# Conditioning matmuls in batches of two k-tiles, and a last output projection that closes one row tile after the other

## The chip, the cores and the metric

The kernel runs on one core of one Trainium2 chip. The time is device microseconds of one execution, the median of several runs. The engines named here are PE (TensorE: matmuls, with PEld for its weight loads), DVE (VectorE), ACT (ScalarE), POOL (GpSimd) and SP (SyncE, which issues the DMAs). Weights come from HBM into SBUF; matmuls write to PSUM, which has eight banks of 128x512 f32.

## The reference

Two layers work on 256 latent and 256 context tokens of width 2048. Cut to what matters here:

```
mod = silu(c) @ ada_w + ada_b              # 2048 -> 6144: shift, scale, gate; also for c_ctx
h   = rms_norm(x, pre_norm) * (1 + scale) + shift
p   = split_columns(h @ w_in)              # one input projection for all branches
att = gqa_attention(q, k, v) * silu(g)     # 8 heads of 128: rows 0 to 7 of the mix (128 columns each)
rw  = rwkv_output(scan fwd + scan bwd) * silu(g)   # 8 heads of 64: rows 8 to 11
pool= pool_mixer(...) * silu(g)            # rows 12 to 15
y   = concat(att, rw, pool) @ w_out        # 2048 -> 2048
x   = x + gate * rms_norm(y, post_norm)
```

The recurrent branch runs four head pairs, the context before the latent tokens; a pair's latent scan starts from the state in which its context scan ends. In the second layer only the latent tokens' output is needed. All is float32.

## The kernel before

The program is written by a list scheduler in Python. Workers (generators: `ada_work`, `main_work`, `front_work`, `back_work`, `scan_work`, `post_work` and others) yield operations; the planner estimates when each could start and takes the earliest, by a priority in steps of 40 ns. What comes out is one fixed order for each engine, and at run time every engine goes through its own order. Buffers are tiles of pools, by class: `wf` (weights as loaded), `sp` (weights split in two), `wa` (conditioning weights), `acc`, `pr`, `scan`, `att`, `ada` (the eight PSUM banks), `y` and so on. PHASES says how many of each class are kept free for it, and the most that it may hold.

The big projections multiply in float32r. A weight tile lands in `wf`, ACT makes a rounded copy (CAST `sp<-wf`), DVE the remainder (TENSOR_TENSOR `sp<-wf,sp`), and three matmuls for each output tile add up the products (high x high, high x low, low x high). This stream, `acc<-h,sp` for the input projections and `acc<-sp,h` for the output projections, is the worker `main`.

The conditioning vectors come from `ada_work`. After the first tiles of layer 0 it walks through 8 parts of 4 x 256 columns, with 16 k-tiles each. A k-tile has two weight tiles `wa` of 128x512, and each makes two matmuls `ada<-wa` with a stationary operand of two columns, into the four strips of 32 rows of one PSUM bank. Before, one k-tile was multiplied as soon as its two tiles were there, in the order in which they were loaded. The array has another form there than in the 128x128 matmuls; the planner holds `ada` matmuls back by 3000 ns of its own time when that form would have to change:

```
HOLD = {None: 1000.0, "ada": 3000.0}
```

The last output projection is two steps, `("out", 1, 1, 0)` and `("out", 1, 1, 1)`: columns 0 to 1023 over all 16 k-tiles, then columns 1024 to 2047. Each holds four PSUM banks (two column tiles `n` by two row tiles `t`). The k-tiles go in the order KMIX, in which the recurrent branch's rows come last: `MIX_ORDER = [0, 1, 2, 3, 6, 7, 4, 5]`. A k-tile's matmuls can't be placed until its row of the mix is there (`self.until("m", l, s, k // 2)`), so in the first step the last two k-tiles (row pair 5, with the last head pair's scan) come after the end of the last scan, and the whole second step after these.

The scan of a head pair (`scan`) has four steps. In each, PE makes `scan<-rf`, ACT copies the result to `sm`, PE makes `scan<-sm,rb`, ACT copies to `rf`, PE makes `scan<-rf,rb`, and DVE updates state and output (`ts`). After the fourth a group norm follows (a reduction, a square on ACT, a `rsqrt` of small DVE steps) and the matmuls `scan<-c,ts`, from which the last rows of the mix are made. `pr<-tp,rb` and `pr<-tp` (32x32) belong to `fin`, which prepares a unit for its scan.

`post_work` closes a projection. For each PSUM bank DVE multiplies by the gate (`y<-acc,y`) and ACT sums the squares (`y,q<-acc`). When all eight are there it takes one `rsqrt` for both row tiles, and for each of eight tiles DVE makes the output (SCALAR_TENSOR_TENSOR `y<-y,q`) and SP writes it.

## Time and profile before

| | us |
|---|---|
| median of 3 runs | 1771.61 (1769.43 to 1776.53) |
| the profiled execution | 1770.03 |
| its span, first to last instruction | 1768.1 |
| PE busy in the span | 1675.5 (95%) |
| DVE busy | 1350.8 (76%) |
| ACT busy | 926.8 (52%) |

The profiled execution's own time is 1.9 us above its span. Busy shares are means over stages with different limits, so a stage is read from a table of its stretch. The ends of matmuls are modelled: their starts are the firm numbers, and the time from one start to the next is what a matmul costs in a stream. A trace shows a program's float32 matmul of this kind as two records (the float32r ones as one): 4 `ada<-wa` of the program are 8 in the trace.

### The profile page before, as it was taken

What the parts mean: (1) busy time and instruction counts of PE and PEld (TensorE: products, weight loads), DVE (VectorE), ACT (ScalarE), POOL (GpSimd) and SP (SyncE); (2) the same over time, 40 slices, a digit from 0 to 9 for tenths busy, and PEclk for the clock granted to TensorE, in tenths of its full rate; (3) what the DMA queues carried; (4) which work ended last, traced back from release to release, by engine and by line L of the source; (5) the groups of instructions that cost most, each with busy time, mean ns of one, the idle gap of its engine ahead of it and who ended that gap; (6) DMA issues with size and microseconds to landing.
All of it is one profiled execution on the core that took longest, in us unless ns stands there. A gap on an engine that the chain in (4) does not pass through costs nothing.

```text
span 1768.1 us, 38232 instructions
## 1 busy us (share of the span) xinstructions
PE 1675.5 (95%) x13658; PEld 1330.3 (75%) x13658; DVE 1350.8 (76%) x4249; ACT 926.8 (52%) x2278; POOL 16.0 (1%) x93
## 2 busy tenths in 40 slices
PE   4999999999999999999999999999999999999977
PEld 3677677666766676667777888899999888888765
DVE  3335888867897869697767685899689999999863
ACT  5324455434554445345446574575455676666541
POOL 0000000000000000000000000000000000000000
PEclk9999999999999999999999999999999999999988
DMA  9993674657364945574669965665434536555642
GB/s 343 362 365 105 206 227 155 225 185 247 120 221 148 277 149 171 170 238 148 207 223 351 328 191 169 199 202 177 147 102 157 155 98 204 153 165 185 215 132 95
DMA packets 218094, 350.03 MB, mean 198 GB/s; under 512 B 22896, under 2 KB 62128, under 8 KB 217904
## 3 DMA queue, kind: packets, MB, share of 16 engines
q1 hardware_dynamic: 217904, 347.60, 60.2%
q8 instruction: 107, 1.75, 0.4%
q14 instruction: 83, 0.68, 0.1%
HBM read 316.54 MB, written 30.97 MB: 197 GB/s over the span
## 4 chain that ended last, share of the span: by engine, by line
PE 72%; DVE 12%; DMA 10%; ACT 2%; issue 2%; SPq 1%; DVEq 0%; POOL 0%; ACTq 0%
PE acc L587 50%; PE scan L587 6%; PE pr L587 5%; PE att L587 5%; PE ada L587 4%; DVE tp L587 3%; DMA wa<-in_ada_w_dram 2%; DVE sp L587 2%; DMA w<-in_ada_w_dram 2%; DVE q L587 1%; DVE rf L587 1%; DMA wf<-in_w_out_dram 1%; DMA wf<-in_w_in_dram 1%; PE st L587 1%; DMA sp<-w 1%
## 5 line engine op out<-in xcount | busy, mean ns | idle before, releaser
L587 PE MATMUL acc<-h,sp 128*128 128x256 f32 (+1 forms) x5088 | 971.1, 339 | 14.1 <-DMA sp<-w 5.6
L587 PEld LDWEIGHTS acc<-h,sp 128*128 128x128 f32 x5088 | 755.4, 190 | 133.9 <-issue 24.3
L587 DVE TENSOR_TENSOR sp<-wf,sp 128x512 fp32r<-128x512 f32 (+1 forms) x568 | 362.4, 664 | 96.4 <-ACT sp L587 90.2
L587 ACT CAST sp<-wf 128x512 fp32r<-128x512 f32 (+1 forms) x624 | 352.3, 603 | 20.8 <-PE acc L587 7.6
L587 PE MATMUL acc<-sp,h 128*128 128x512 f32 x1152 | 284.6, 403 | 2.9 <-DVE sp L587 2.9
L587 PEld LDWEIGHTS acc<-sp,h 128*128 128x128 f32 x1152 | 216.9, 191 | 54.1 <-DVE sp L587 3.8
L587 DVE TENSOR_TENSOR tp<-tp 128x48 f32<-128x48 f32 (+23 forms) x552 | 133.3, 247 | 5.6
L587 DVE TENSOR_TENSOR tp<-dt,tp 128x48 f32<-128x48 f32 (+23 forms) x496 | 112.0, 226 | 5.6
L587 PE MATMUL ada<-wa,cs 128*2 128x256 f32 x1024 | 85.8, 380 | 6.3 <-DMA wa<-in_ada_w_dram 6.2
L587 ACT CAST pw<-pw 128x512 fp32r<-128x512 f32 x56 | 34.8, 621 | 71.8 <-DMA pw<-in_w_in_dram 59.2
L587 ACT COPY sm<-scan 128x128 f32<-128x128 f32 x64 | 17.0, 265 | 104.4 <-PE scan L587 104.0
L587 DVE TENSOR_TENSOR rf<-tp 64x256 f32<-64x256 f32 x176 | 70.2, 421 | 0.4
L587 DVE STREAM_TRANSPOSE dt<-tp 128x1024 f32<-128x1024 f32 x32 | 65.7, 2077 | 0.0
L587 ACT ACTIVATE aq<-att,q 128x512 f32<-128x512 f32 (+1 forms) x48 | 33.9, 707 | 59.8 <-DVE q L587 49.7
L587 ACT COPY rf<-scan 64x128 f32<-64x128 f32 x128 | 33.2, 259 | 55.6 <-PE scan L587 50.8
L587 DVE SCALAR_TENSOR_TENSOR q<-q 128x4 f32<-128x4 f32 (+3 forms) x378 | 58.3, 159 | 4.2
L587 PEld LDWEIGHTS scan<-rf 128*64 128x64 f32 x896 | 37.3, 137 | 26.2 <-issue 9.2
L587 PE MATMUL ada<-w,cs 128*2 128x128 f32 x1024 | 37.0, 296 | 20.5 <-DMA w<-in_ada_w_dram 19.6
L587 DVE COPY adasb<-ada 2x128 f32<-2x128 f32 (+1 forms) x32 | 11.4, 357 | 57.4 <-ACT adasb L587 50.9
L587 DVE TENSOR_TENSOR pw<-pw 128x512 f32<-128x512 f32 x56 | 38.5, 687 | 21.6 <-ACT pw L587 21.3
L587 PE MATMUL scan<-rf 128*64 128x64 f32 x896 | 49.3, 230 | 4.4 <-DVE rf L587 4.1
L587 ACT COPY tp<-rb 32x128 f32<-32x128 f32 x128 | 37.5, 295 | 28.4 <-DVE rb L587 26.9
(154 smaller groups left out, 1965.7 us busy)
## 6 DMA issues: line engine op xcount, KB each, us to landing
wf<-in_w_in_dram SPq DMA_DIRECT2D x384, 256.0 KB, 3.8
wa<-in_ada_w_dram SPq DMA_DIRECT2D x256, 256.0 KB, 4.2
wf<-in_w_out_dram SPq DMA_DIRECT2D x192, 256.0 KB, 4.5
w<-in_ada_w_dram SPq DMA_DIRECT2D x128, 256.0 KB, 5.3
pw<-in_w_in_dram SPq DMA_DIRECT2D x56, 256.0 KB, 4.8
w<-pw SPq DMA_DIRECT2D x56, 256.0 KB, 2.5
sp<-w SPq DMA_DIRECT2D x56, 256.0 KB, 3.2
wf<-in_w_in_dram SPq DMA_DIRECT2D x48, 128.0 KB, 4.4
```

The costliest lines, as they stand in the source:

```text
L587: op.call(**op.args)
```

## The change

Conditioning: in the parts of 256 columns `ada_work` takes ADA_BATCH = 2 k-tiles at a time (the first eight parts, of 128 columns, stay). It waits until the planner has issued all four tiles, multiplies the k-tile that was loaded last first, and frees all four together. Its window in the planner, now 8 * ADA_BATCH, is 16 operations as before.

The last projection: one step `("end", 1, 1)` with worker functions `main_end` and `post_last`. ENDING[0] has 14 k-tiles for all four column tiles (columns 0 to 1023 by k-tile, then column tile 2, then 3); ENDING[1] the last two k-tiles for all four. All eight PSUM banks are held at the end. In ENDING[1] row tile 0 is multiplied first, the split weights are held, and row tile 1 follows from them. `post_last` closes row tile 0 with a `rsqrt` of its own, then row tile 1. The class `sp` may now hold 30 tiles in the phase "last" (4 kept before, at most 24), `y` keeps 18. When the last unit's `fin`, scan and attention are through, `done(pr=0, ...)`, `done(scan=0)` and `done(att=0, ...)` give their PSUM banks free.

In the diff, the additions of `("end", 1, 1)` to STEPS, `main_work` and `run`, the class limits and the three calls of `done` are left out.

```diff
     "between": {"pw": 2, "wf": 6, "wa": 0, "sp": (8, 16), "y": 1, "h": 32, "acc": 4, "st": 0, "ada": 0, "rf": 14, "rb": 5, "lo": 4, "at": 4, "aq": 6},
     "turn": {"y": 14, "h": 34, "acc": 4, "st": 1, "ada": 0, "pr": 2, "scan": 1, "att": 0, "rf": 9, "rb": 5, "lo": 4, "at": 0, "aq": 0},
     "second": {"sp": (4, 11), "tp": 16, "ta": 7, "tl": 0, "y": 1, "h": 32, "acc": 2, "ada": 0, "st": 0, "pr": 2, "scan": 2, "att": 1, "rf": 12, "rb": 5, "lo": 4, "at": 8, "aq": 6},
-    "last": {"h": 16, "y": 14, "sp": 4, "acc": 4, "rf": 14, "rb": 5, "lo": 4, "at": 4, "aq": 6},
+    "last": {"h": 16, "y": 18, "sp": (4, 30), "acc": 4, "rf": 14, "rb": 5, "lo": 4, "at": 4, "aq": 6},
 }
 
 
...
 UNITS = [[(g, s) for g in range(4) for s in range(2)], [(0, 0), (1, 0), (2, 0), (0, 1), (1, 1), (3, 0), (2, 1), (3, 1)]]
 MIX_ORDER = [0, 1, 2, 3, 6, 7, 4, 5]
 KMIX = [2 * p + i for p in MIX_ORDER for i in range(2)]
+ENDING = [[(k, n) for k in KMIX[:14] for n in (0, 1)] + [(k, n) for n in (2, 3) for k in KMIX[:14]], [(k, n) for n in range(4) for k in KMIX[14:]]]
 STREAMS = {"w": (0, 1), "c": (0,), "l": (1,)}
 ADA_SINGLE = ((0, 0), (0, 1))
 ADA_FIRST = [(0, quad, [r]) for r in range(4) for quad in range(2)]
 ADA_REST = [(l, q, [2 * h, 2 * h + 1]) for l, q in ((0, 2), (1, 0), (1, 1), (1, 2)) for h in range(2)]
 ADA_RATE = 7
+ADA_BATCH = 2
 LEND = ("at",)
 AHEAD = (1, 2)
 SLOT = 40.0
...
                 for q in range(4):
                     for _, _, cb, _, bs in GROUPS(l)[at[0]]:
                         yield from self.w_tile(l, cb, bs, q)
+            elif kind == "end":
+                for k, n in ENDING[0] + ENDING[1]:
+                    w = yield Alloc("wf", (128, 1, 512))
+                    yield self.D.dma_start(out=w[:, 0], in_=self.a["w_out"][l, 128 * k:128 * k + 128, 512 * n:512 * n + 512])
+                    self.push(self.wq, (w, None, 0))
             else:
                 for k in KMIX:
                     for i in range(2):
...
         for l, quad, part in ADA_FIRST + ADA_REST:
             n = 128 * len(part)
             ps = yield Alloc("ada", (128, 512))
-            for k in range(KT):
-                yield Until(lambda: len(self.adaq) > 0)
-                for i in range(len(part)):
-                    if i:
-                        yield Until(lambda: len(self.adaq) > 0)
-                    w = self.adaq.pop(0)
-                    for j in range(4) if n == 128 else (2 * i, 2 * i + 1):
-                        rhs = w[:, j, :] if n == 128 else w[:, :, j % 2, :]
-                        yield T.matmul(out=ps[32 * j:32 * j + 2, 0:n], lhsT=self.cs[:, k, :], rhs=rhs, start=(k == 0), stop=(k == KT - 1))
-                    self.free(w)
+            size = 1 if n == 128 else ADA_BATCH
+            for k0 in range(0, KT, size):
+                ws = []
+                for _ in range(size * len(part)):
+                    yield Until(lambda: len(self.adaq) > 0)
+                    ws.append(self.adaq.pop(0))
+                for z in range(size):
+                    k = k0 + size - 1 - z
+                    for i in range(len(part)):
+                        w = ws[len(part) * (k - k0) + i]
+                        for j in range(4) if n == 128 else (2 * i, 2 * i + 1):
+                            rhs = w[:, j, :] if n == 128 else w[:, :, j % 2, :]
+                            yield T.matmul(out=ps[32 * j:32 * j + 2, 0:n], lhsT=self.cs[:, k, :], rhs=rhs,
+                                           start=(k0 == 0 and z == 0), stop=(k0 + size == KT and z == size - 1))
+                self.free(*ws)
             sb = self.adasb
             for j in range(4):
                 if j % 2:
...
         if nh == 1:
             self.free(*self.mx[l, s][0].values(), *self.mx[l, s][1].values())
 
+    def main_end(self, l, s):
+        T = self.T
+        self.nmain += 64
+        self.flag("end")
+        ps, held = {}, []
+
+        def product(k, n, t, h, w):
+            mh, ml = (self.mx[l, s][j][k // 2][:, k % 2, 128 * t:128 * t + 128] for j in range(2))
+            if (n, t) not in ps:
+                ps[n, t] = yield Alloc("acc", (128, 512))
+            yield T.matmul(out=ps[n, t], lhsT=mh, rhs=h[:, 0], start=(k == KMIX[0]), stop=False)
+            yield T.matmul(out=ps[n, t], lhsT=mh, rhs=w[:, 0], start=False, stop=False)
+            yield T.matmul(out=ps[n, t], lhsT=ml, rhs=h[:, 0], start=False, stop=(k == KMIX[-1]))
+
+        for late in range(2):
+            for k, n in ENDING[late]:
+                yield Until(lambda: len(self.sq) > 0)
+                h, w = self.sq.pop(0)
+                yield self.until("m", l, s, k // 2)
+                for t in range(2 - late):
+                    yield from product(k, n, t, h, w)
+                    if late and k == KMIX[-1]:
+                        self.sch.defer(lambda key=(l, s, n, t), p=ps[n, t]: self.yq.__setitem__(key, p))
+                if late:
+                    held.append((k, n, h, w))
+                else:
+                    self.free(h, w)
+        for k, n, h, w in held:
+            yield from product(k, n, 1, h, w)
+            self.free(h, w)
+            if k == KMIX[-1]:
+                self.sch.defer(lambda key=(l, s, n, 1), p=ps[n, 1]: self.yq.__setitem__(key, p))
+        self.free(*self.mx[l, s][0].values(), *self.mx[l, s][1].values())
+
+    def post_last(self):
+        V, S, G, T, D_ = self.V, self.S, self.G, self.T, self.D
+        l, s = DEPTH - 1, 1
+        yield self.until("end")
+        yield self.until("gp", l)
+        gp = []
+        for n in range(4):
+            g = yield Alloc("y", (128, 512))
+            src = self.gpd[l].rearrange("(k s) p -> s k p", s=2)[s, 4 * n:4 * n + 4, :]
+            yield D_.dma_start(out=g.rearrange("p (k c) -> p k c", k=4), in_=src.unsqueeze(0).to_broadcast([128, 4, 128]))
+            gp.append(g)
+        acc = yield Alloc("q", (128, 2, 4))
+        for t in range(2):
+            xr, y = [], []
+            rows = slice(128 * t, 128 * t + 128)
+            for n in range(4):
+                z = yield Alloc("y", (128, 512))
+                yield D_.dma_start(out=z, in_=self.x1d[rows, 512 * n:512 * n + 512])
+                xr.append(z)
+            for n in range(4):
+                yield Until(lambda: (l, s, n, t) in self.yq)
+                ps = self.yq.pop((l, s, n, t))
+                z = yield Alloc("y", (128, 512))
+                yield V.tensor_tensor(out=z, in0=ps, in1=gp[n], op=ALU.mult)
+                junk = yield Alloc("y", (128, 512))
+                yield S.activation(out=junk, in_=ps, func=AF.Square, accum_out=acc[:, t, n:n + 1])
+                self.free(junk, ps)
+                y.append(z)
+            ss = yield Alloc("q", (128, 1))
+            yield V.tensor_reduce(out=ss, in_=acc[:, t], axis=AX.X, op=ALU.add)
+            yield V.tensor_scalar(out=ss, in0=ss, scalar1=1.0 / D, scalar2=EPS, op0=ALU.mult, op1=ALU.add)
+            rs = yield from self.rsqrt(ss, 1)
+            for n in range(4):
+                yield V.scalar_tensor_tensor(out=y[n], in0=y[n], scalar=rs, in1=xr[n], op0=ALU.mult, op1=ALU.add)
+                self.free(xr[n])
+                yield D_.dma_start(out=self.a["out"][0, rows, 512 * n:512 * n + 512], in_=y[n])
+                self.free(y[n])
+            self.free(ss, rs)
+        self.free(acc, *gp)
+
     def emit(self, l, kind, i, ps, mode):
         self.push(self.eq if kind in ("lora", "r", "rk", "rv") else self.aq, (l, kind, i, ps, mode))
 
...
             UB = []
         self.push(self.pq, (l, g, s, need, RS, W, UB, W2, Z, PC, bv))
 
+    def done(self, **least):
+        self.sch.defer(lambda: self.sch.set_phase(least))
+
     def scan_work(self):
         yield self.until("consts")
         state = {}
...
```

How the order on PE changes in layer 0, in a scan of the recurrent branch. Before (`ada<-wa` x4 is one k-tile, x8 a batch of two; `acc<-h,sp` is the main stream):

```order
L587 MATMUL scan<-rf 64x64 x8
L587 MATMUL ada<-wa,cs 2x256 x4
L587 MATMUL scan<-sm,rb 64x64 x4
L587 MATMUL acc<-h,sp 128x512 x7
L587 MATMUL ada<-wa,cs 2x256 x4
L587 MATMUL scan<-rf,rb 64x64 x8
L587 MATMUL acc<-h,sp 128x512 x8
L587 MATMUL scan<-rf 64x64 x8
```

The same kind of place now:

```order
L589 MATMUL scan<-rf 64x64 x8
L589 MATMUL acc<-h,sp 128x512 x7
L589 MATMUL scan<-sm,rb 64x64 x4
L589 MATMUL ada<-wa,cs 2x256 x8
L589 MATMUL scan<-rf,rb 64x64 x8
L589 MATMUL acc<-h,sp 128x512 x8
L589 MATMUL scan<-rf 64x64 x8
L589 MATMUL acc<-h,sp 128x512 x7
```

Two lone k-tiles with other work between them have become one run of two k-tiles between two scan matmuls.

How the order on PE changes at the end of the program. Before, the last unit's scan and the rest of the last projection:

```order
L587 MATMUL acc<-sp,h 128x512 x9
L587 MATMUL scan<-rf 64x64 x8
L587 MATMUL scan<-sm,rb 64x64 x4
L587 MATMUL scan<-rf,rb 64x64 x8
L587 MATMUL scan<-rf 64x64 x8
L587 MATMUL scan<-sm,rb 64x64 x4
L587 MATMUL scan<-rf,rb 64x64 x8
L587 MATMUL scan<-rf 64x64 x8
L587 MATMUL scan<-sm,rb 64x64 x4
L587 MATMUL scan<-rf,rb 64x64 x4
L587 MATMUL scan<-c,ts 64x64 x8
L587 MATMUL acc<-sp,h 128x512 x216
```

And now:

```order
L589 MATMUL scan<-rf,rb 64x64 x8
L589 MATMUL acc<-sp,h 128x512 x9
L589 MATMUL scan<-rf 64x64 x8
L589 MATMUL acc<-sp,h 128x512 x7
L589 MATMUL scan<-sm,rb 64x64 x4
L589 MATMUL acc<-sp,h 128x512 x7
L589 MATMUL scan<-rf,rb 64x64 x8
L589 MATMUL scan<-rf 64x64 x8
L589 MATMUL scan<-sm,rb 64x64 x4
L589 MATMUL scan<-rf,rb 64x64 x4
L589 MATMUL scan<-c,ts 64x64 x8
L589 MATMUL acc<-sp,h 128x512 x132
```

The main stream goes on until the third step's `scan<-sm,rb`, where it ended ahead of the second step's `scan<-rf`; 132 of its matmuls are left behind the scan, where there were 216.

ACT in the same scan steps (`sm<-scan` and `rf<-scan` are the scan's copies, `sp<-wf` the splits of weights, the ACTIVATE `ts<-ts` the square of the group norm). Before:

```order
L587 COPY sm<-scan 128x128
L587 COPY rf<-scan 64x128 x2
L587 COPY sm<-scan 128x128
L587 COPY rf<-scan 64x2x64 x2
L587 COPY sm<-scan 128x128
L587 COPY rf<-scan 64x2x64 x2
L587 ACTIVATE ts<-ts 128x256
```

And now:

```order
L589 COPY sm<-scan 128x128
L589 CAST sp<-wf 128x512 x2
L589 COPY rf<-scan 64x2x64 x2
L589 CAST sp<-wf 128x512
L589 COPY sm<-scan 128x128
L589 CAST sp<-wf 128x512 x3
L589 COPY rf<-scan 64x2x64 x2
L589 CAST sp<-wf 128x512 x2
L589 ACTIVATE ts<-ts 128x256
```

Splits of weights now stand between the scan's copies. On DVE, too, there are now three `sp<-wf,sp` ahead of the last sum `ts<-ts,scan` and two between it and its reduction, where there were none.

How DVE closes the output. Before, with buffer numbers, from the first product of the second step on:

```order
L587 TENSOR_TENSOR y_23544<-acc_23181,y_23162 128x512
L587 TENSOR_TENSOR y_23548<-acc_23189,y_23163 128x512
L587 TENSOR_TENSOR y_23546<-acc_23186,y_23162 128x512
L587 TENSOR_TENSOR y_23550<-acc_23199,y_23163 128x512
L587 TENSOR_REDUCE q_23552<-q_23164 128x2
L587 TENSOR_SCALAR q_23552<-q_23552 128x2
L587 TENSOR_SCALAR q_23554<-q_23552 128x2
L587 TENSOR_SCALAR q_23553<-q_23554 128x2
L587 SCALAR_TENSOR_TENSOR q_23554<-q_23553 128x2
```

And now, from the middle of row tile 0's `rsqrt` on (`y_23559`, `y_23566`, `y_23572`, `y_23580` are the products of row tile 1, `y_23496` and the like the tiles of row tile 0):

```order
L589 TENSOR_TENSOR y_23572<-acc_22946,y_22289 128x512
L589 TENSOR_TENSOR q_23529<-q_23529,q_23527 128x1
L589 TENSOR_TENSOR y_23580<-acc_23350,y_22290 128x512
L589 SCALAR_TENSOR_TENSOR q_23528<-q_23529,q_23528 128x1
L589 SCALAR_TENSOR_TENSOR q_23529<-q_23528 128x1
L589 TENSOR_TENSOR q_23529<-q_23529,q_23527 128x1
L589 SCALAR_TENSOR_TENSOR q_23528<-q_23529,q_23528 128x1
L589 SCALAR_TENSOR_TENSOR y_23496<-y_23496,q_23528,y_22292 128x512
L589 TENSOR_REDUCE q_23583<-q_22291 128x1
L589 SCALAR_TENSOR_TENSOR y_23506<-y_23506,q_23528,y_22293 128x512
L589 SCALAR_TENSOR_TENSOR y_23518<-y_23518,q_23528,y_22294 128x512
L589 SCALAR_TENSOR_TENSOR y_23525<-y_23525,q_23528,y_22295 128x512
```

The products of row tile 1 stand in between the steps of row tile 0's `rsqrt`, and row tile 0's output tiles come after them; row tile 1's reduction, too, stands ahead of three of these.

## Rows read from the trace of the kernel before

**Rows 1.** The page's busy times: us, share of the span, instructions.

```profile
PE 1675.5 (95%) x13658; PEld 1330.3 (75%) x13658; DVE 1350.8 (76%) x4249; ACT 926.8 (52%) x2278; POOL 16.0 (1%) x93
```

**Rows 2.** Busy us by stretch (x instructions), then clock, DMA share, GB/s.

```profile
800.00:900.00 100.00, 99.78 (x827) 73.02 (x826) 76.45 (x243) 49.93 (x127) 0.53 (x1) 1.00 0.53 168
...
1400.00:1500.00 100.00, 93.29 (x923) 83.73 (x924) 93.81 (x364) 68.45 (x188) 1.78 (x9) 1.00 0.47 148
1640.00:1680.00 40.00, 40.00 (x372) 29.80 (x368) 31.67 (x108) 19.00 (x48) 0.00 (x0) 1.00 0.59 193
1680.00:1720.00 40.00, 31.16 (x228) 24.39 (x227) 24.01 (x61) 17.85 (x44) 0.00 (x0) 0.83 0.41 129
...
1704.00:1708.00 4.00, 4.00 (x11) 3.15 (x10) 2.94 (x6) 2.20 (x5) 0.00 (x0) 0.54 0.28 73
```

**Rows 3.** The tile `wa`: its instructions, who waited for it (us, times), landing.

```profile
L587 PE MATMUL ada<-wa,cs x1024: 377/378/634, 172.7 to 882.9; 128*2 128x256 f32 x171
...
  PEld ada L587: 14.1, 21
...
  PE ada L587: 6.2, 7
...
DMA to landing us min/median/max: 2.6/4.2/6.9
```

**Rows 4.** PE in order of time, layer 0: start, duration, what [idle before].

```profile
407.03 1.70 PE L587 MATMUL ada<-wa,cs 128*2 128x256 f32 x16
408.65 6.99 PE L587 MATMUL acc<-h,sp 128*128 128x512 f32 x29
...
427.23 0.61 PE L587 MATMUL ada<-wa,cs 128*2 128x256 f32 x8
427.77 0.73 PE L587 MATMUL acc<-h,sp 128*128 128x512 f32 x2
...
434.70 1.04 PE L587 MATMUL ada<-wa,cs 128*2 128x256 f32 x16
435.68 0.65 PE L587 MATMUL pr<-tp 32*32 32x32 f32 x32
```

**Rows 5.** PE in order of time, 680 to 688 us.

```profile
682.39 0.61 PE L587 MATMUL ada<-wa,cs 128*2 128x256 f32 x8 [1.69 <-DMA wa<-in_ada_w_dram]
685.23 1.02 PE L587 MATMUL ada<-wa,cs 128*2 128x256 f32 x4 [2.22 <-DMA wa<-in_ada_w_dram]
```

**Rows 6.** PE in order of time, the end of the program.

```profile
1645.28 2.11 PE L587 MATMUL acc<-sp,h 128*128 128x512 f32 x8
1647.33 0.69 PE L587 MATMUL scan<-rf 128*64 128x64 f32 x16
...
1669.46 8.84 PE L587 MATMUL acc<-sp,h 128*128 128x512 f32 x37
1678.23 0.45 PE L587 MATMUL scan<-rf 128*64 128x64 f32 x8
...
1685.04 0.69 PE L587 MATMUL scan<-rf 128*64 128x64 f32 x16
...
1690.95 1.10 PE L587 MATMUL scan<-rf,rb 128*64 128x64 f32 x16 [0.36 <-ACT rf L587]
...
1702.57 52.73 PE L587 MATMUL acc<-sp,h 128*128 128x512 f32 x216
```

**Rows 7.** ACT and DVE in order of time, the end of the program.

```profile
1704.03 2.18 ACT L587 CAST sp<-wf 128x512 fp32r<-128x512 f32 x4
1704.67 2.50 DVE L587 TENSOR_TENSOR sp<-wf,sp 128x512 fp32r<-128x512 f32 x4
...
1754.40 2.80 DVE L587 TENSOR_TENSOR y<-acc,y 128x512 f32<-128x512 f32 x4 [23.21 <-PE acc L587]
...
1757.12 0.15 DVE L587 TENSOR_REDUCE q<-q 128x2 f32<-128x8 f32 x1
...
1759.68 5.39 DVE L587 SCALAR_TENSOR_TENSOR y<-y,q 128x512 f32<-128x512 f32 x8
```

More of the change, by code (lines that the diff above doesn't have):

```diff
@@ L173, in STEPS @@
     out = [("out", 0, 0, 0), ("out", 0, 0, 1), ("out", 0, 1, 0)]
-    return into[0] + out + into[1][:EARLY] + [("out", 0, 1, 1)] + into[1][EARLY:] + [("out", 1, 1, 0), ("out", 1, 1, 1)]
+    return into[0] + out + into[1][:EARLY] + [("out", 0, 1, 1)] + into[1][EARLY:] + [("end", 1, 1)]
 def TILES_IN(l, gi):
@@ L1116, in main_work @@
                 yield from self.main_in(l, at[0], left)
+            elif kind == "end":
+                yield from self.main_end(l, *at)
             else:
@@ L1289, in fin_work @@
             yield from self.fin(*self.zq.pop(0))
+        self.done(pr=0, rf=0, rb=0, lo=0)
     def front(self, l, g, s, up):
@@ L1528, in scan_work @@
                 self.phase("rested", "first")
+        self.done(scan=0)
     def scan(self, Sc, l, g, s, need, RS, W, UB, W2, Z, PC, bv):
@@ L1696, in att_work @@
                     self.free(*self.kf[l, i // 4], *self.vf[l, i // 4])
+        self.done(att=0, at=0, aq=0)
     def gate_work(self):
@@ L1917, in run @@
         sch.add("mix", PRIO["mix"], self.mix_work())
-        for l in range(DEPTH):
-            for s in PASSES(l):
-                sch.add("post%d%d" % (l, s), PRIO["post"], self.post_work(l, s), 16)
+        for s in PASSES(0):
+            sch.add("post0%d" % s, PRIO["post"], self.post_work(0, s), 16)
+        sch.add("postend", PRIO["post"], self.post_last(), 16)
         sch.add("load", PRIO["load"], self.loads())
-        sch.add("ada", PRIO["ada"], self.ada_work(), 16)
+        sch.add("ada", PRIO["ada"], self.ada_work(), 8 * ADA_BATCH)
         sch.add("wl", PRIO["wl"], self.w_loads())
```

2 rows, old and new, of the table CLASSES are left out of this document.

## Prediction

> **What bounds the kernel now.** I read the page's busy times first, then a table of busy time by stretch, then TensorE's timeline at three places and the timeline of all engines at the end. TensorE (PE) is busy 95% of the span and VectorE (DVE) 76% [rows 1]. The average hides stages. In 800 to 900 us, inside layer 0, PE is busy 99.78 of 100 us and DVE 76.45. In 1400 to 1500, inside layer 1, PE has 93.29 and DVE 93.81: there the two stand level. In 1640 to 1680 PE is busy all 40 us. In 1680 to 1720 it loses nearly nine, and the granted clock is 0.83 [rows 2]. So layer 0 is bound by the stream of matmuls, whatever takes PE's time there costs its full length, and the only long hole late in the program lies just before 1702.57 [rows 6].
>
> **The change part by part.** It has two parts that meet only through the planner, which orders everything again from the first `wa` matmul on.
>
> *Conditioning in batches.* No matmul is added or removed: 1024 records [rows 3] are 128 k-tiles of 8 records (4 program matmuls each). What changes is how often the array leaves its 128x128 form for the strips of two columns. By the order there are 112 unbroken runs of `ada<-wa` before and 72 now. What one run costs: a lone k-tile takes 427.77 - 427.23 = 0.54 us to the next start, and two in a row take 435.68 - 434.70 = 0.98 [rows 4]. Two lone ones would take 1.08, so joining a pair saves 0.10 us. Forty runs fewer are 4.0 us.
>
> The main stream is cut less often too: `acc<-h,sp` at 128x512 stands in 290 runs before and 271 now. What a cut costs follows from two runs of like matmuls: 8 take 1647.33 - 1645.28 = 2.05 us and 37 take 1678.23 - 1669.46 = 8.77 [rows 6]. That gives 6.72 / 29 = 0.232 us for one matmul and 2.05 - 8 x 0.232 = 0.20 for each run. Nineteen runs fewer are 3.8 us.
>
> Third, the waits for the weights. PE sat idle for a landing `wa` tile 6.2 us at 7 places, and its weight loader 14.1 us at 21 [rows 3]. These lie mostly in runs of several k-tiles: the one at 407.03 holds two and takes 408.65 - 407.03 = 1.62 us, 0.64 over the clean pair, while the lone tile at 427.23 waits for nothing [rows 4]. The code tells why: the planner holds `ada` work back (HOLD) only at the change of the array's form, so the first k-tile of a run starts well after its weights, and a second one that follows in the same form starts as soon as the planner believes it has landed. Before, 25 runs hold more than one k-tile. Now no run is longer than one batch, and a batch begins with its last loaded k-tile, so the hold covers nearly all of it. I bound this term by 14.1 us saved on one side and, on the other, by nothing saved and a loss (the slow rival below). I take the 6.2 us of PE's own idle time, since the loader's waits partly lie beside running matmuls. The stretch at half clock that could follow such waits (1.69 and 2.22 us at 680 to 685 [rows 5]) I leave out of the sum.
>
> Each `wa` transfer is still one issue on SP; there are 256 in both. Behind a waiting batch on PE stands everything else, the main stream included.
>
> *The last projection.* Two things are to be costed: the hole before the last mix rows, and the closing.
>
> Before, PE has 168 `acc` matmuls that don't need the last row pair. It runs out of them at 1685.04 with three of the last unit's four scan steps to go, and starts again at 1702.57: 17.53 us [rows 6]. Now 252 stand ahead of the end of the scan. By the order the hole begins two steps later, at the third step's `scan<-rf,rb`, which started at 1690.95: 1702.57 - 1690.95 = 11.62 us. Not all of the difference is gained. Five groups of scan matmuls that stood in the hole now cut the dense stream, at up to 0.69 us each (the 16-record one at 1647.33) [rows 6], 3.4 us, and make five more runs of `acc`, 1.0 us. That leaves 17.53 - 11.62 - 4.4 = 1.5 us. Against it stands what the larger `sp` pool lets in: splits of weights now stand on ACT and DVE inside the chain of the last step, where none stood. On DVE two come between the last `ts` sum and its reduction, at 2.50 / 4 = 0.62 us each, and on ACT three come between the copies `sm` and `rf`, 2.18 / 4 = 0.55 each [rows 7]; about half of the latter fits into the time until the matmul ends. That is 1.25 + 0.85 = 2.1 us. I take 0 for the hole: 2.5 gained (no split in the way) to 2.5 lost (all of them).
>
> In the hole the clock falls. PE ran 11 matmuls in 1704 to 1708 at 0.54 [rows 2], 0.36 us each, where 0.232 is the rule at full clock; some 12 matmuls lose about 2 us in all. The Trainium skill, "TensorE: Matmul & The Clock Gate", in "Why this matters for your kernels", advises against idle gaps between bursts of matmuls, since the clock drops to half after them. By that rule a hole that shrinks enough would give the 2 us back. Against it, the order leaves the idle stretch of the group norm just ahead of 1701.52 in place, so I let the loss stand.
>
> The closing. Before, the last matmul ends at 1702.57 + 52.73 = 1755.30 [rows 6] and DVE's last output tile at 1759.68 + 5.39 = 1765.07 [rows 7], 9.77 us later. Now row tile 0 is to be closed while row tile 1 still multiplies. But DVE's order has the four products of row tile 1 in between the steps of row tile 0's `rsqrt`: the last of them, `y_23580<-acc_23350`, needs the very last matmul, and behind it stand four small steps, all four output products of row tile 0, and the whole of row tile 1. DVE takes its work in order: at 1754.40 it stood 23.21 us idle at the head of its queue [rows 7]. So after the last matmul come: about 0.2 us until the product before it is done, one product (2.80 / 4 = 0.70), 4 small steps at (1759.68 - 1757.12) / 13 = 0.197, one output product at 5.39 / 8 = 0.67, a reduction, three output products, 12 small steps, four output products: 0.2 + 0.70 + 0.79 + 0.67 + 0.20 + 2.02 + 2.36 + 2.70 = 9.64 us. The last output transfer follows as it did. The closing is worth 0.1 us. If the three early output products and the rest of row tile 0 were out of the way, it would be 0.2 + 0.70 + 0.20 + 2.36 + 2.70 = 6.16, and 3.6 us gained.
>
> On DVE's order the Trainium skill, "TensorE: Matmul & The Clock Gate", in the table at its head, has VectorE's queue as strict first in, first out. By that rule, too, the early closing is lost; without it the sum would be 3.6 us lower.
>
> *Sum.* 4.0 + 3.8 + 6.2 + 0 + 0.1 = 14.1 us saved. The profiled execution took 1770.03 us around its span of 1768.1, so 1756; the median of the runs shown is 1771.61, 1.6 above it. I predict 1757.
>
> **The rivals.**
>
> *Given back in layer 1.* PE gets ahead of the recurrent chain and then waits for it. For it: DVE is as busy as PE in 1400 to 1500 [rows 2], and in the order `pr<-tp,rb`, which opens the finish of the unit before the last, stood behind one `acc` of the last projection and now stands behind 36. Against it: layer 1 as a whole starts earlier too, so the chain moves along. If those 35 matmuls at 0.232 are only waited for elsewhere, 8.1 us come back: 1765.
>
> *Slower: late batches.* A batch can't start until four tiles have landed, where before two sufficed; the pool keeps only four `wa` tiles for certain, so the next batch's transfers may wait for this batch's matmuls, and a transfer takes 4.2 us to land [rows 3]. PE waits in order with the main stream behind. For it: runs of two k-tiles waited 0.64 us at 407.03 and 1.69 and 2.22 at 680 to 685 [rows 4, 5]. Against it: 76 of the 112 runs before were lone k-tiles, mostly like the clean one at 427.23. With a mean wait w over 64 batches the change is -7.9 + (64w - 6.2): it is slower than before from w = 0.22 us on. At 0.5 us, less than at 407.03, it gives 1770 + 18 = 1788, 1789 beside the median.
>
> *The end is not bound by PE.* If the last unit's scan ends when it did, whatever PE does beside it, then 84 of the 216 matmuls behind it are gone, 84 x 0.232 = 19.5 us, beside the 14 of layer 0: about 1738. Against it: PE has no idle time in 1640 to 1680 [rows 2].
>
> *Row tile 0 closes early after all,* if DVE reaches its steps before the products of row tile 1 are ready: 3.6 us less, 1753. The order speaks against it.
>
> **How the numbers follow.** The forecast holds with 0.50, its own range 1748 to 1764 (the waits between 0 and 14.1 us, the hole 2.5 either way). Given back in layer 1: 0.27; late batches: 0.12; the end not bound by PE: 0.08; the early close: 0.03. What can be told from no change is 0.5%, 8.9 us, so faster means under 1762.8. Faster: 0.43 of the forecast's 0.50, the 0.11 of the last two, and 0.05 of the give-back: 0.59. Slower: 0.10 of the late batches and 0.02 of the give-back: 0.12. Same: the rest, 0.29. The range is 1744 to 1771.
>
> **What would show it.** In the changed profile: `ada<-wa` in some 72 runs with PE idle on `wa` of 2 us or less at its places; PE's busy time some 8 us lower; the layers' turn about 14 us earlier. At the end: a hole of 11 to 14 us with a stretch at half clock at its end, and 9 to 10 us from the last matmul to DVE's last output product, with an output product of row tile 0 behind the last product from PSUM. I am wrong if PE waits for `wa` as long as before, if new idle time stands at `pr` or `scan` in layer 1, or if the last matmul comes more than 20 us earlier.

## The result, and the profile after

The changed kernel takes 1783.07 us (median of 6 runs, 1780.34 to 1788.42) where the kernel before takes 1770.82 in the same comparison: a ratio of 1.0067 (95% interval 1.0046 to 1.0088), 12 us slower. 1757 was predicted. The profiled execution took 1780.94 us around a span of 1779.2. The busy times of the whole program, the answer to [rows 1]:

```profile
PE 1670.7 (94%) x13658; PEld 1339.7 (75%) x13658; DVE 1352.5 (76%) x4263; ACT 931.4 (52%) x2279; POOL 15.9 (1%) x93
```

PE is busy 4.8 us less than before, in a span that is 11.1 us longer: it sits idle 16 us more. Who waited for the tile `wa` (us, times), the answer to [rows 3]:

```profile
L589 PE MATMUL ada<-wa,cs x1024: 376/379/634, 177.4 to 874.0; 128*2 128x256 f32 x171
...
  PEld ada L589: 6.4, 8
...
  PE ada L589: 2.9, 4
```

PE waits 3.3 us less for `wa` than before, as the prediction wanted in direction. The busy time by stretch, columns as in [rows 2], first layer 0, then the turn between the layers, then layer 1:

```profile
150.00:880.00 730.00, 714.18 (x5594) 520.28 (x5593) 584.42 (x1919) 358.82 (x904) 7.49 (x46) 0.99 0.61 194
900.00:970.00 70.00, 62.24 (x303) 47.11 (x298) 50.17 (x97) 42.34 (x85) 0.00 (x0) 0.96 0.89 294
...
1400.00:1500.00 100.00, 89.59 (x863) 80.97 (x862) 84.85 (x324) 61.07 (x165) 1.75 (x8) 0.91 0.41 126
```

The columns after the times are the granted clock (1.00 is 2.4 GHz, 0.50 is 1.2 GHz, called half clock below), the DMA share and GB/s. In layer 0 PE is idle 730 - 714.18 = 15.8 us. The same stretch before:

```profile
150.00:880.00 730.00, 717.56 (x5578) 508.79 (x5576) 579.75 (x1907) 353.52 (x894) 7.50 (x46) 0.99 0.60 191
900.00:970.00 70.00, 67.91 (x334) 53.25 (x333) 51.95 (x100) 42.49 (x86) 0.00 (x0) 0.98 0.92 314
```

It was idle 12.4 us there. So 3.3 us less on `wa`, and still 3.4 us more in all: PE waits for DVE and ACT in other places of layer 0. At the turn it is idle 7.8 us (before 2.1). In 1400 to 1500 PE and DVE are both less busy than before, and the clock is 0.91.

PE at the turn, in order of time. Before:

```profile
927.71 36.89 PE L587 MATMUL acc<-sp,h 128*128 128x512 f32 x157
966.69 23.59 PE L587 MATMUL acc<-sp,h 128*128 128x512 f32 x94 [2.09 <-DVE sp L587]
```

And after:

```profile
925.64 11.38 PE L589 MATMUL acc<-sp,h 128*128 128x512 f32 x48
937.48 8.11 PE L589 MATMUL acc<-sp,h 128*128 128x512 f32 x34 [0.45 <-ACT sp L589]
950.27 12.96 PE L589 MATMUL acc<-sp,h 128*128 128x512 f32 x48 [4.68 <-ACT h L589]
963.39 1.25 PE L589 MATMUL acc<-sp,h 128*128 128x512 f32 x4 [0.17 <-ACT sp L589]
966.92 23.39 PE L589 MATMUL acc<-sp,h 128*128 128x512 f32 x93 [2.28 <-DVE sp L589]
```

PE arrives ahead of its old place. It waits 4.68 us for `h` (the last row of the mix, read back from DRAM), then 2.28 us for a split weight, and goes on at 966.92, where it went on at 966.69 before. The lead can be read at two matmuls of this stream. At the 151st, behind which PE has done the same work in both, it is 948.0 - 941.3 = 6.7 us; at the 241st (973.0 and 973.2) it is gone. Up to 1350 us the two profiles run within 2 us of each other.

What ended the last wait stands on DVE. Before, then after:

```profile
963.55 2.48 DVE L587 TENSOR_TENSOR y<-acc,y 128x512 f32<-128x512 f32 x4 [0.56 <-PE acc L587]
965.95 3.10 DVE L587 TENSOR_TENSOR sp<-wf,sp 128x512 fp32r<-128x512 f32 x5
```

```profile
963.79 2.48 DVE L589 TENSOR_TENSOR y<-acc,y 128x512 f32<-128x512 f32 x4
966.18 3.69 DVE L589 TENSOR_TENSOR sp<-wf,sp 128x512 fp32r<-128x512 f32 x6
```

PE waits for the split of the 37th tile of w_out. The tile had landed at 960.6 before and at 952.2 in the changed kernel, so its loading is not what the wait ended with. Its split on DVE stands behind the four products `y<-acc,y` that close the first half of the projection, and these cannot start before their gate, `y<-gpd`, has landed (963.5 and 962.0); in the changed kernel DVE comes to them 1.8 us later still, after `h<-y,h` of the mix. PE goes on 0.05 and 0.06 us after the split is done.

Layer 1, all engines in order of time around the longest new gap:

```profile
1457.16 0.63 PE L589 MATMUL acc<-h,sp 128*128 128x256 f32 x3
...
1463.30 3.85 DVE L589 STREAM_TRANSPOSE dt<-tp 128x1024 f32<-128x1024 f32 x2
...
1465.77 1.69 PE L589 MATMUL att<-aq,at 128*128 128x256 f32 x12
...
1467.08 0.24 DVE L589 TENSOR_TENSOR ts<-ts,scan 128x128 f32<-128x128 f32 x1
...
1474.10 0.41 DVE L589 TENSOR_TENSOR ts<-ts,q 128x256 f32<-128x256 f32 x1
...
1474.65 1.12 PE L589 MATMUL scan<-c,ts 64*64 64x64 f32 x16 [7.20 <-DVE tp L589]
```

The group norm of a unit runs on DVE from 1467.08 to 1474.5. It began late, behind two transposes, and nothing stands between on PE's order: `scan<-c,ts` is next, and the main stream has had no matmul since 1457.16. PE idles 7.20 us, and half clock follows:

```profile
1470.00:1486.00 16.00, 11.35 (x68) 10.59 (x69) 12.58 (x67) 6.92 (x19) 0.00 (x0) 0.50 0.10 26
```

Two more such waits, 2.34 at `scan<-rf` and 3.88 at `pr<-tp,bonesr`, stand at 1597 to 1603, again with half clock behind them. The last projection starts 13 us later than before (1643.0 against 1629.9). All of layer 1, before and then after:

```profile
1000.00:1640.00 640.00, 616.42 (x5360) 560.15 (x5360) 552.80 (x1787) 397.95 (x994) 7.77 (x40) 0.99 0.54 171
```

```profile
1000.00:1640.00 640.00, 610.69 (x5232) 557.43 (x5230) 539.49 (x1753) 392.01 (x974) 7.70 (x40) 0.97 0.51 162
```

Idle time rises from 23.6 to 29.3 us, and the mean clock falls from 0.99 to 0.97, which over 640 us is 13 us of work at full clock. Together that is more than the 13 us that are lost, so part of the slow stretches cost nothing.

PE at the end, the answer to [rows 6], and DVE's closing, the answer to [rows 7]:

```profile
1720.74 0.83 PE L589 MATMUL scan<-rf,rb 128*64 128x64 f32 x16
...
1725.25 0.97 PE L589 MATMUL scan<-rf,rb 64*64 64x64 f32 x8 [1.26 <-ACT rf L589]
1732.63 1.12 PE L589 MATMUL scan<-c,ts 64*64 64x64 f32 x16 [6.41 <-DVE ts L589]
1733.68 11.68 PE L589 MATMUL acc<-sp,h 128*128 128x512 f32 x45
```

```profile
1765.56 0.69 DVE L589 TENSOR_TENSOR y<-acc,y 128x512 f32<-128x512 f32 x1
...
1766.94 0.75 DVE L589 SCALAR_TENSOR_TENSOR y<-y,q 128x512 f32<-128x512 f32 x1
...
1771.96 2.74 DVE L589 SCALAR_TENSOR_TENSOR y<-y,q 128x512 f32<-128x512 f32 x4
```

The hole is 1733.68 - 1720.74 = 12.9 us (11.62 worked out). The last matmul ends at 1765.5, DVE's last output tile at 1774.70: 9.2 us (9.64 worked out), with row tile 0's first output tile behind the last product, as the order said.

### The profile page after: what moved, and what is told of

Same layout as the page of the kernel before. It is cut to its first block, busy times and chain, and to the rows that moved or that the text cites. A ratio compares the mean times of both kernels' runs of the same rounds, so it can differ in the third digit from the quotient of the medians.

```text
span 1779.2 us, 38253 instructions
## 1 busy us (share of the span) xinstructions
PE 1670.7 (94%) x13658; PEld 1339.7 (75%) x13658; DVE 1352.5 (76%) x4263; ACT 931.4 (52%) x2279; POOL 15.9 (1%) x93
## 4 chain that ended last, share of the span: by engine, by line
PE 73%; DVE 11%; DMA 9%; ACT 4%; issue 2%; SPq 1%; DVEq 0%; ACTq 0%
PE acc L589 51%; PE pr L589 6%; PE scan L589 6%; PE att L589 5%; PE ada L589 4%; DVE tp L589 2%; DMA w<-in_ada_w_dram 2%; DVE sp L589 2%; DMA pw<-in_w_in_dram 1%; DVE q L589 1%; ACT sp L589 1%; DMA wa<-in_ada_w_dram 1%; DMA sp<-w 1%; DVE rf L589 1%; PE st L589 1%
## 5 line engine op out<-in xcount | busy, mean ns | idle before, releaser
L589 PE MATMUL acc<-h,sp 128*128 128x256 f32 (+1 forms) x5088 | 966.5, 338 | 12.4 <-DVE h L589 5.1
L589 PE MATMUL acc<-sp,h 128*128 128x512 f32 x1152 | 289.8, 405 | 8.6 <-ACT h L589 4.7
L589 DVE TENSOR_TENSOR tp<-tp 128x48 f32<-128x48 f32 (+24 forms) x552 | 132.6, 245 | 6.0 <-ACT tp L589 0.6
L589 PE MATMUL ada<-wa,cs 128*2 128x256 f32 x1024 | 75.3, 385 | 3.2 <-DMA wa<-in_ada_w_dram 2.9
L589 ACT ACTIVATE tp<-tp 128x256 f32<-128x256 f32 x80 | 30.5, 412 | 44.3 <-DVE tp L589 43.6
L589 ACT CAST aq<-att 128x256 fp32r<-128x256 f32 x80 | 28.1, 374 | 47.5 <-PE att L589 46.5
```

The lines of the kernel that those rows point to most:

```text
L589: op.call(**op.args)
```

## The experiments

Theory: the two parts are separate. The new end gains a little; the batches save PE time in layer 0, which is lost at the turn; and the planner, which orders all of layer 1 anew, happens on an order that costs 12 us more. The ratios are to the kernel before, run beside each version, with 95% intervals.

**One part alone (e1, e2).** e1 is the changed kernel with single k-tiles, e2 the kernel before with batches:

```diff
-ADA_BATCH = 2
+ADA_BATCH = 1
-        sch.add("ada", PRIO["ada"], self.ada_work(), 8 * ADA_BATCH)
+        sch.add("ada", PRIO["ada"], self.ada_work(), 16)
```

> The changed kernel with conditioning one k-tile at a time again (ADA_BATCH 1, window 16), the new end kept. Its order on PE is that of the kernel before up to the last projection, so everything up to 1600 us must read as before. Theory (two separate parts, the batching's reordering costs about 13 us up to the start of the last projection, the new end gives some 2 us back): 1767 to 1770, no half clock around 1467, first last-projection matmul at 1630 within 1 us of before. Rival (the new pool limits and the new end themselves cost the time, the batching is harmless): 1778 or more.

> The kernel before with conditioning in batches of two k-tiles, the old end kept. Its order on PE is that of the changed kernel up to the last projection. Theory: layer 0 some 12 us ahead at 911 us, level again at 970, 13 us behind at the first matmul of the last projection, and 1782 to 1786 at the end. Rival (the new end costs the time): 1758 to 1765.

e1: 1766.98 us, ratio 0.9983 (0.9971 to 0.9995). e2: 1785.61, ratio 1.0076 (1.0062 to 1.009). So the end gains 3.0 us, and all of the loss comes with the batches. In e2 the gap ahead of `scan<-c,ts` is there again (7.22 us, until 1481.79), in e1 it is not.

**What the turn waits for (e3, e4).** Row pair 4 in place of 5, in the changed kernel (e3) and the one before (e4):

```diff
-                yield self.until("m", l, s, k // 2)
-                mh, ml = (self.mx[l, s][j][k // 2][:, k % 2] for j in range(2))
+                p = 4 if (l, s, nh) == (0, 0, 0) and k // 2 == 5 else k // 2
+                yield self.until("m", l, s, p)
+                mh, ml = (self.mx[l, s][j][p][:, k % 2] for j in range(2))
```

> The changed kernel, but in the first half of layer 0's first output projection the last two k-tiles multiply row pair 4 of the mix in place of row pair 5, so nothing there waits for the last head pair's scan and its way through DRAM (the result is wrong by that). Read at matmul 241 of acc<-sp,h (973.0 us before and 973.2 in the changed kernel). Theory A (the turn is bound by the last mix row's chain, 4.7 us idle and what follows): the 12 us of layer 0 survive, that matmul starts at 961 to 966. Theory B (the turn is bound by the loading of w_out, DMA share about 1): it starts at 971 to 974. The total beyond that point depends on the order the planner finds for layer 1, and tells nothing.

> The kernel before with the same edit (row pair 4 for row pair 5 in the first half of layer 0's output projection, result wrong by that); the order on every engine stays. Both theories: no change, 1768 to 1773, and the same 2 us of idle time at 965 us, since PE had matmuls enough there until the row came. If it were faster by over 4 us, the last mix row bound the kernel before too.

PE of e3 at the turn:

```profile
949.15 10.96 PE L589 MATMUL acc<-sp,h 128*128 128x512 f32 x46 [0.95 <-ACT sp L589]
961.88 1.42 PE L589 MATMUL acc<-sp,h 128*128 128x512 f32 x4 [1.76 <-ACT sp L589]
966.52 8.86 PE L589 MATMUL acc<-sp,h 128*128 128x512 f32 x31 [3.23 <-DVE sp L589]
```

The wait for `h` is gone, PE waits longer for split weights, and goes on at 966.52 all the same; the 241st matmul comes at 972.7. Theory A falls: the splits bind by themselves. That theory B is right does not follow: the 37th tile has landed at 954.6, and again its split (965.78) stands on DVE behind the closing products (963.38), which start when their gate lands, at 963.3. The edit also leaves the last row's way through DRAM in the orders of SP, ACT and DVE. e4 (1773.58, one run) is unchanged, with its 2.04 us at 964.3.

**Layer 1's order alone (e5, e6).** From layer 1's first matmul on, the planner takes a recorded order in place of its own choice:

```diff
+            if self.replay or any(nd.key == PLAN_FROM for nd in self.ready_nodes.values()):
+                ...
+                nd = min(self.ready_nodes.values(), key=lambda x: self.rank.get(x.key, -1))
```

> The changed kernel, both parts, up to the first matmul of layer 1; from there the planner issues every operation in the order of run e1 (which is that of the kernel before up to the last projection, then the new end). So batching in layer 0 with the old order of layer 1. Theory (the batches cost nothing themselves, the 13 us are lost in the new order that the planner finds for layer 1, and layer 0's gain is lost at the turn): level with e1, 1764 to 1769, half clock around 1467 gone. Rival (the batches themselves cost the time): 1778 or more. Rival (layer 0's gain survives once layer 1 is as before): 1756 to 1761.

> The reverse: run e1 (conditioning one k-tile at a time, the new end) up to the first matmul of layer 1, and from there every operation in the order of the changed kernel. Theory: the order alone costs what the changed kernel lost, 1778 to 1784, with idle time of about 7 us ahead of scan<-c,ts near 1467 and half clock behind it. Rival: 1765 to 1769, as e1.

e5: 1770.1, ratio 0.9989 (0.9974 to 1.0004). e6: 1782.26, ratio 1.0047 (1.0031 to 1.0064). One stretch of layer 1, first e5, then e6, which has no batches:

```profile
1400.00:1500.00 100.00, 93.72 (x925) 83.95 (x925) 95.21 (x368) 66.44 (x182) 1.89 (x10) 1.00 0.47 149
```

```profile
1400.00:1500.00 100.00, 90.48 (x872) 82.20 (x872) 84.41 (x325) 61.00 (x164) 1.75 (x8) 0.91 0.42 128
```

With the old order batches cost nothing in layer 1; with the new order the kernel without batches has the changed kernel's row. The order alone is worth 1.0047 - 0.9983 = 0.64%, 11 us. Against e1, e5 also shows that the batches as they stood gain nothing that can be told: the intervals around 0.9989 and 0.9983 overlap.

**The turn set free (e7, e8, e9).** An early split (`pw`) is a weight of layer 1 that is loaded, split by ACT and DVE and stored again during layer 0; 14 of the 56 stores fall in the loading of w_out. In the changed kernel SP, which issues its DMAs in order, issued nothing from 918.9 to 925.6; for the last 5.5 us it waited, at such a store, until DVE had made the split:

```profile
918.48 0.38 SPq L589 DMA_DIRECT2D pw<-in_w_in_dram  x1
925.58 0.33 SPq L589 DMA_DIRECT2D w<-pw  x1
```

Behind it stand the loads of w_out. e7 (on e5) and e8 (on e1) make these splits earlier; e9 (on e5) leaves them where they are and issues them on POOL:

```diff
-SPLIT_RATE = 4
+SPLIT_RATE = 3
-    "between": {"pw": 2, "wf": 6, "wa": 0, ...
+    "between": {"pw": 0, "wf": 6, "wa": 0, ...
```

```diff
-                yield self.D.dma_start(out=w, in_=self.a["w_in"][l, q, cb // 2][:, 2 * i:2 * i + 2, :])
+                yield self.G.dma_start(out=w, in_=self.a["w_in"][l, q, cb // 2][:, 2 * i:2 * i + 2, :])
...
-                yield self.D.dma_start(out=self.low[key][i], in_=w.rearrange(flat))
+                yield self.G.dma_start(out=self.low[key][i], in_=w.rearrange(flat))
```

> As e5, but the early splits of layer 1's weights (pw) come at three tiles of the main stream each in place of four (SPLIT_RATE 3, and no pw tiles kept in phase between), so all 56 are done before the loading of w_out starts, where 14 stood in it. Theory C (their loads and stores in SP's queue and on the DMA engines hold up w_out at the turn, so PE waits for split weights at 965 whatever its lead): no wait there, first matmuls of layer 1 some 5 to 8 us ahead of the kernel before, 1757 to 1763. Rival (w_out's own loading binds): as e5 within 2 us.

> As e1 (no batches, new end, order of e1 from the first matmul of layer 1), with the early splits moved as in e7. Theory C: the 2 us wait at 965 and the half clock behind it go, 2 to 4 us under e1: 1763 to 1766. Rival: as e1. Either way e7 against e8 is the batches alone with the turn free: by theory C 5 to 8 us, by the rival none.

> As e5 (batches, new end, old order of layer 1), but the loads and stores of the early splits (pw) are issued by POOL in place of SP; their number and bytes stay. Theory S (at the turn SP's queue is what holds w_out up: a store w<-pw stands at its head until ACT and DVE have made the split): no wait of PE for sp at 965, first matmuls of layer 1 5 to 8 us ahead of the kernel before, 1756 to 1762 as e7. Theory D (the bytes on the DMA engines hold it up): wait as in e5, 1767 to 1772.

e7: 1758.17, ratio 0.9919 (0.9896 to 0.9943). e8: 1766.33, ratio 0.9962 (0.9949 to 0.9976). e9: 1764.18, ratio 0.9958 (0.9944 to 0.9973). PE of e7 at the turn, then of e9:

```profile
924.13 51.08 PE L619 MATMUL acc<-sp,h 128*128 128x512 f32 x219
```

```profile
932.72 8.19 PE L623 MATMUL acc<-sp,h 128*128 128x512 f32 x34
950.90 24.43 PE L623 MATMUL acc<-sp,h 128*128 128x512 f32 x97 [9.99 <-ACT h L623]
```

In e7 PE runs through without a wait, and so it does in e8. In e9, whose time lies between the ranges of its two theories, the wait at 965 is gone too, with the same DMAs, but PE waits 9.99 us for the last mix row, in which time the splits can be made; so e9 doesn't separate S from D. e13 takes that wait away too, by e3's edit:

> As e9 (early splits issued by POOL), with the edit of e3: the last two k-tiles of the first half of layer 0's first output projection multiply row pair 4 of the mix in place of row pair 5, so PE doesn't wait for the last mix row (the result is wrong by that). Against e3, where SP issues the early splits and PE waits for split weights 1.8 us at 960 and 3.2 at 963. Theory S (SP's order): PE runs through 940 to 975 with under 1 us of waiting for sp, and layer 1 starts 8 us or more ahead of the kernel before. Theory D (the bytes): it waits some 5 us for sp as in e3, and goes on near 966.

PE of e13 (1752.13 us, one run):

```profile
928.81 19.25 PE L623 MATMUL acc<-sp,h 128*128 128x512 f32 x82
949.15 1.24 PE L623 MATMUL acc<-sp,h 128*128 128x512 f32 x4 [1.09 <-ACT sp L623]
953.55 31.77 PE L623 MATMUL acc<-sp,h 128*128 128x512 f32 x129 [3.16 <-DVE sp L623]
```

PE waits 4.3 us for splits, so S's "under 1 us" is wrong, and goes on at 953.55, 13 us before e3, so D's 966 is wrong too. But e13 doesn't decide between them, since most of its lead on e3 is older than the turn. At the 151st matmul of `acc<-sp,h`, with the same work behind PE, e13 stands at 932.6 and e3 at 943.4: 10.8 us apart. The orders of layer 0 differ between the two from 175 us on, and the granted clock up to 900 us is 0.991 in e13 and 0.983 in e3; 0.008 of 900 us is some 7 us. From the 151st to the 241st matmul e7 takes 20.9 us, e13 27.2 and e3 29.3. At the turn itself, then, the other queue gave 2 us of the 8.4 that e3 loses there. The landings agree: 50 us after the first load of w_out 31 tiles have landed in e13 and 23 in e3, but the 37th, the one that PE waits for, lands 71.3 and 72.7 us after it. In e13 SP stands 17.7 us, until 929.4, at another store, `ygd<-tp`, with loads of w_out behind it. The Trainium skill, "DMA: Bandwidth & Descriptors", "Issuing engines are not separate DMA queues", has it that DMAs issued from several engines save only the time to initiate them, which is usually small. The 2 us here don't contradict it.

Theories S and D both have the loading of w_out as the limit, and that is the weak point. DVE in e13, then in e7:

```profile
950.20 2.69 DVE L623 TENSOR_TENSOR y<-acc,y 128x512 f32<-128x512 f32 x4 [3.33 <-ACT sp L623]
952.81 2.49 DVE L623 TENSOR_TENSOR sp<-wf,sp 128x512 fp32r<-128x512 f32 x4
```

```profile
957.17 2.48 DVE L619 TENSOR_TENSOR y<-acc,y 128x512 f32<-128x512 f32 x4 [2.03 <-DMA y<-gpd]
959.57 3.09 DVE L619 TENSOR_TENSOR sp<-wf,sp 128x512 fp32r<-128x512 f32 x5
```

In e13 the 37th tile had landed at 940.1, 13 us before PE goes on; its split waits for the closing products, and these for their gate (landed at 950.1). In e7 the order on DVE is the same, but the gate lands at 957.1, 8.5 us earlier than in e5 (965.6), and the split is done at 960.25, before PE comes to the tile at 961.11. What e7 and e8 show is that moving the early splits clears the turn. These take SP's queue, the DMA engines, ACT (0.62 us each) and DVE (0.69 us each); which of them held the closing back no run takes apart, and it stays open.

With the turn free, the batches gain 8.2 us (e7 against e8; by the two intervals some 3 to 12).

**What a batch saves, and the closing (e10, e11).** Both on e7, with PE's order of e7 in e10:

```diff
-        sch.add("postend", PRIO["post"], self.post_last(), 16)
+        sch.add("postend", PRIO["post"], self.post_last(), 3)
```

```diff
-                    k = k0 + size - 1 - z
+                    k = k0 + z
```

> As e7, but the worker that closes the output may hold 3 operations in place of 16, so that on DVE all of row tile 0's rsqrt and output tiles stand ahead of row tile 1's products (PE's order is that of e7). By the prediction's rival (row tile 0 closes early) 6.2 us from the last matmul to the last output tile in place of 9.2, and some 3 us less than e7: 1755. Rival: DVE's own work after row tile 0's last product (2 times 2.4 us of rsqrt, 8 output tiles of 0.67, 4 products of 0.68, some 13 us) is what ends last, whatever its order: 9 to 10 us, 1757 to 1759.

> As e7, but a batch multiplies its first loaded k-tile first. By the order its two k-tiles then often part: ada<-wa stands in 103 runs in place of 67, and the main stream acc<-h,sp at 128x512 in 292 in place of 263. Theory (each run costs what was read before, 0.10 us for ada and 0.20 for the main stream): 36 x 0.10 + 29 x 0.20 = 9.4 us more than e7, 1765 to 1769. Rival (what a batch saves is PE's waiting for wa, not the runs): idle time on wa well over e7's 8.2 us, and the same number of us lost; or no loss at all, 1756 to 1760.

e10: 1757.26, ratio 0.9916 (0.9903 to 0.9928). e11: 1766.96, ratio 0.9969 (0.9958 to 0.998). e11 is 9.7 us slower than e10 (some 6 to 12 by the intervals), and 9.4 were expected from 36 and 29 more runs; PE's idle time on `wa` is about the same in both (6.3 and 6.1 us). So the gain of a batch goes with fewer runs and not with the waits for `wa`. The agreement to 0.3 us is in part luck: e10 also has the other closing, and PE's whole idle time in 150 to 880, which the sum leaves out, is 16.1 us in e10 and 12.5 in e11. DVE closing e10:

```profile
1739.95 2.74 DVE L619 SCALAR_TENSOR_TENSOR y<-y,q 128x512 f32<-128x512 f32 x4
1742.61 2.47 DVE L619 TENSOR_TENSOR y<-acc,y 128x512 f32<-128x512 f32 x4
...
1748.36 2.74 DVE L619 SCALAR_TENSOR_TENSOR y<-y,q 128x512 f32<-128x512 f32 x4
```

Row tile 0 does close first, and from the last matmul (ends at 1740.5) to the last output tile it takes 10.6 us, where e7 takes 9.2: row tile 0's output tiles now hold up row tile 1's products on DVE. So it is DVE's own work, as the rival had it. e10 and e7 can't be told apart (0.9916 and 0.9919); both are some 14 us under the kernel before, the fastest versions with the right result.

**An edit without meaning (e12).** On the kernel before:

```diff
-HOLD = {None: 1000.0, "ada": 3000.0}
+HOLD = {None: 1000.0, "ada": 3300.0}
```

> The kernel before with one number of the planner changed: it holds conditioning matmuls back by 3300 ns of its own time in place of 3000. No batches, old end; the planner orders everything again, layer 1 too. Theory (any edit ahead of layer 1 draws a new order for it, and these differ by many us for no reason of their own): off the kernel before by more than 4 us in either direction, most of it between 1350 and 1640 us. Rival (orders drawn anew are alike, and it was the batches that led to a bad one): 1768 to 1774.

1790.17 us, ratio 1.0101 (1.0085 to 1.0116). Its row of the same stretch:

```profile
1400.00:1500.00 100.00, 86.69 (x840) 75.60 (x842) 88.28 (x351) 56.06 (x154) 1.75 (x8) 0.84 0.38 118
```

18.6 us slower with neither part of the change. Layer 1 starts at 1054.6 us (1055.4 before), so the loss lies behind that. One new order can cost many us for reasons that have nothing to do with the edit that drew it.

## Why the prediction was wrong

- **Runs of `ada` and of the main stream, 4.0 + 3.8 us: borne out.** The trace has the 72 and 271 runs. The price per run fits twice: e11 against e10 9.7 us for 9.4 worked out; e8 (110 and 285 runs) against e7 (67 and 263) 8.2 for 43 x 0.10 + 22 x 0.20 = 8.7. Both differences are known to 3 to 5 us only.
- **Waits for `wa`, 6.2 us: wrong, and it turned round.** In four profiles with the old order of layer 0 (before, e1, e4, e6) PE waits 6.2, 6.9, 7.6 and 8.7 us for `wa`, in four with the new one (after, e2, e3, e5) 2.9, 6.6, 2.9 and 3.5: 3.4 saved in the mean. But all idle time in 150 to 880 is 12.4, 14.4, 11.5 and 14.8 before and 15.8, 18.0, 16.0 and 16.0 now. The new order makes PE wait 6.5 us more for DVE and ACT elsewhere. The term was not 6.2 saved but 3.2 lost, and layer 0's gain 7.8 - 3.2 = 4.6 where I had 14. Read directly, at the 151st matmul of `acc<-sp,h`, the four new profiles are 4.2 us ahead in the mean (944.5 against 948.7). The 6.7 us of the pair above is luck in part: two profiles with the same order on PE, e7 and e10, lie 8.6 us apart there.
- **The step that failed: "the layers' turn about 14 us earlier", and a sum carried from layer 0 to the end.** I asked what layer 0 saves and never what stands behind it. The turn did not come earlier: the 241st matmul stands at 973.2 (973.0 before), and layer 1's first matmul at 1055.6 (1055.4). The 2.09 us wait at 966.69 was there to be read: a split on DVE, behind the closing products and their gate's load, set that point and not PE. With the early splits out of the way (e7 against e8) the lead stays: layer 1 starts at 1049.6 and 1054.8.
- **Layer 1: the largest term, 11 us, and it had none in the sum.** I let the new order there count for nothing on the argument that the chain moves along. My rival "given back in layer 1" named the stage and gave it 8.1 us, at `pr<-tp,rb`. The time went at other places, `scan<-c,ts` above all, and by another way: not a chain that did not move along, but a new order that leaves PE without main-stream matmuls while DVE does a group norm. e6 shows that it needs no batches, e2 that it needs no new end, and e12 that a bad order can come with neither. New idle time at `scan` in layer 1 is one of the signs I had named against me.
- The rule of the Trainium skill that I weighed at the end ("TensorE: Matmul & The Clock Gate", "Why this matters for your kernels": idle gaps between bursts bring half clock) agrees with the rows here, and mattered more in layer 1: behind the 7.2 us gap the clock is 0.50 for 16 us.
- **The end, 0.1 us: 3.0 us gained (0.9 to 5.1).** The closing was nearly right; the hole, taken at 0, was sized too low. From the start of the last projection to the end of the last matmul it is 122.6 us where it was 125.4; from there to DVE's last tile 9.2 for 9.8; from that to the end of the span 4.5 for 3.0, the output's transfers, which I had left as they were. Why they take longer was not tried.
- The rivals: late batches fall, since PE waits less for `wa`; "the end is not bound by PE" falls, since the scan ended 31 us later than before, with the stream beside it (23.5 in e1, with the old layer 1); an early close gains nothing that can be told (e10).

## What to carry to other kernels

Time saved in one stage reaches the end only through the next stage's limit, so read the first wait behind the saving (here a split on DVE behind other work in the planner's order, and a row's way through DRAM) before adding it to a sum. Where a planner orders everything anew, a change is two things, the edit and a new draw of the order; hold the order of the untouched part fixed to measure the edit, and change something without meaning to see how wide the draws are (here 18.6 us, more than either part). A late arrival that an edit seems to cure must be read from the same work on: most of e13's 13 us were there before the stage that it was to mend. The edit may then be worth having after all: with layer 1's order kept and the early splits out of the turn it makes 1758 us.

## What the runs showed of the hardware

Three things I had not expected. A gap of 7.2 us on PE was followed by a granted clock of 0.50 for 16 us, with PE busy 11.35 of them; full clock would have done that work in about half the time, so the gap may have cost up to 7.2 + 5.7 = 12.9 us, an estimate. The same order on PE is not the same time: e7's profile and e10's have it and part by 8.6 us in layer 0, where the granted clock from 150 to 880 us is 0.984 and 0.995. And a store whose data are late holds back the loads behind it in SP's order: 5.5 us in the changed kernel, 17.7 in e13.
